# Bonus products three steps later, and the norms' products in another PSUM bank

## The chip, the cores and the metric

The kernel runs on one core of a Trainium2 chip. Times are microseconds (us) on the device, from the first to the last instruction of one execution with what lies around them. Matmuls run on TensorE (PE), elementwise work on VectorE (DVE), ScalarE (ACT) and GpSimd (POOL); SyncE (SP) and ACT issue the transfers. The engines run side by side, each through its own list of instructions in order, and wait for one another by semaphores. TensorE accumulates into PSUM banks, which the other engines read out.

## The reference

Two layers over 2048 tokens of width 1024, everything in float32. Layer 0 is RWKV-7 time mixing: shifted inputs are projected to r, k, v and g, a decay and a removal rate come from small LoRA products, and a recurrence over the tokens updates one 64 x 64 state for each of 16 heads. Beside the state's output each token gets a bonus from its own key and value:

```
y = ((y - mu) * lax.rsqrt(var + GN_EPS)).reshape(B, S, D) * ln_g + ln_b
bonus = jnp.sum(r * k * r_k, axis=-1, keepdims=True) * v
y = (y + bonus.reshape(B, S, D)) * jax.nn.silu(g)
```

Then one K and one V are projected from the residual stream, after a norm over each token. Layer 1 is attention with three groups of query heads (windows 128, 512 and 2048, with strides 1, 4 and 16) over this K and V, merged by their softmax sums, gated and projected back.

## The kernel before

A float32 product is done as three products of halves that the PE takes at full rate (`mm3`, L73 to L75: high times high, low times high, high times low). The kernel has three phases.

**Phase 1** (to about 1085 us) projects r, k, v and g, over four blocks of 512 tokens each. One step of this dense work is one slice of the contraction, into two banks: six products of 128x512. Beside it the loop drives a background: `run()` does 16 preps, `prep(v, hb)`, for eight blocks `v` of 256 tokens and two halves `hb` of the heads. A prep goes on by one yield in each dense step, and the tuple `W` (L37) says how many steps it waits between its stages. The stages of one prep:

- the second LoRA products L531 and L532, first for the decay (tile `sw`, weights `wa`), then for the removal rate (tile `tha`, weights `wb`); ACT takes each tanh of them, L535
- on DVE the running sum of the decays L537 and L540, on ACT their exponentials L544 and L545
- the products L550 that spread the keys' norms, and DVE's L553 to L559 which normalise and scale the keys
- POOL's L565, and L568 which writes r times k over the tile `kn`; on DVE L566, L570 and L569, which write the tiles `ar` and `bk`
- 64 pairs of short products of `ar` and `bk`, 32x32 each, L583 (called block products here); ACT copies their bank out, L599, into a tile of the pool slot of `sw`; two steps later they are stored to `abD`, L591
- the bonus: four products of `kn` with the weights r_k, L606, a copy on ACT, L608, and two steps later the turn, two transposes L614, which DVE's L618 copies into `beta`

All PSUM banks of the preps come from a pool of three, named "z". The tile `sw` has one buffer, so the tanh of the next prep waits until `abD` is stored.

Short things are not issued at once. A queue `tiny` holds them, and `sprinkle(2)` issues two after each pair of dense products. `later(steps, f, "prep")` puts f on a list of due times, counted in dense steps; `catch_up` issues what is due, and `catch_up("prep")` all of that name at once. Another background, the eliminations L640 and L642 (a triangular inverse by rows), runs on DVE and POOL between the preps.

**Phase 2** (about 1085 to 1780 us) runs the recurrence in chunks of 64 tokens and projects its output. The first chunk starts with L882.

**Phase 3** projects K, V, three sets of queries and the gate (jobs "k", "v", 2, 1, 0, "gate"), and runs the attention beside it. A job's products go into a pool of two banks, "ps". K's rows are turned by transposes L1458 into the one bank "tr", ACT copies them out (L1478) and issues their stores itself (L1472, and the larger L1481 with 16 values in a row). V's banks are copied out by ACT in L1486. Between the last token block of K and the one before the last of V, each block's tokens are scaled for the layers that follow: `rstd(tb)` spreads the 256 norms over all partitions by two products with the identity (L1331) into the bank "tr", ACT copies them out (L1334), POOL multiplies (L1318), DVE scales and shifts (L1322), and ACT issues the store `xbT` (L1324).

What stands where in an engine's list is not the order of the program text: a list scheduler takes the program in text order, keeps a model of each engine and of the banks, and orders each engine's list by it.

Of the kernel before, what the change touches and what calls it, by code (L numbers as in the profile page):

```python
# [9 lines left out]
F32 = mybir.dt.float32  # L10
# [5 lines left out]
P = 128  # L16
# [33 lines left out]
class Trunk:  # L50
# [148 lines left out]
    def phase1(self, keep):  # L199
# [17 lines left out]
        with ExitStack() as ctx:  # L217
# [12 lines left out]
            pz = bpool("pz", 3, space=PSUM)  # L230
# [227 lines left out]
            tiny, elims, due = deque(), deque(), []  # L458

            def sprinkle(n):  # L460

                while tiny and n:
                    tiny.popleft()()
                    n -= 1
# [5 lines left out]
            def catch_up(which=None):  # L470
                for d in sorted(due, key=lambda d: d[0]):
                    if d[0] <= now[0] or which in (d[2], "all"):
                        due.remove(d)
                        d[1]()

            def open_prep():
# [27 lines left out]
                def wait(n):  # L504
                    for _ in range(n):
                        yield
# [16 lines left out]
                def prep(v, hb, hr, kt, rt):  # L523
                    sw, tha = tile("sw"), tile("tha")
                    for i, dst in ((0, sw), (1, tha)):
                        for g in range(2):
                            z = pz.tile([P, 2, 256], F32, name="z")
# [18 lines left out]
                    for g in range(2):  # L546
                        z = pz.tile([P, 2, 256], F32, name="z")
# [10 lines left out]
                    nc.vector.scalar_tensor_tensor(k2, k2, 1.0, kt, op0=ALU.add, op1=ALU.mult)  # L558
                    nc.vector.scalar_tensor_tensor(tha, tha, 1.0, kn, op0=ALU.add, op1=ALU.mult)  # L559
                    yield from wait(W[3])  # L560
                    sprinkle(99)
                    catch_up("prep")
                    ar, bk = big("ar"), big("bk")
# [47 lines left out]
                    def turn(bo):  # L611
# [3 lines left out]
                        for s in range(2):  # L615
                            for c in range(2):
                                dst = self.beta[rows[1 - s]].rearrange("p (b c) j -> p c b j", c=2)
                                nc.vector.tensor_copy(dst[:, c, 2 * v:2 * v + 2, 4 * hb:4 * hb + 4], z[rows[c], :, :, s])  # L618
                    tiny.append(bonus)

                def eliminate(v, tiles=None):

# [39 lines left out]
                def run():  # L662
                    for v in range(NV):
                        for hb in range(2):
                            while v >= 2 * keys[0]:
                                yield
                            tiles = loads(v, hb)
                            yield from wait(W[0])
                            yield from prep(v, hb, *tiles)
                            yield from wait(W[6])  # L670
                    sprinkle(99)
# [554 lines left out]
    def phase3(self, keep):  # L1226
# [8 lines left out]
        with ExitStack() as ctx:  # L1235
            pool = lambda name, bufs, **kw: ctx.enter_context(tc.tile_pool(name=name, bufs=bufs, **kw))
            kept = self.kept
            wst, pp, pt, xb_, xp = (kept[n] for n in ("wst", "pp", "pt", "xb", "xs"))
# [6 lines left out]
            def two(which):  # L1245
                n = {"yp": "yc", "zp": "zc"}[which]
                return kept[which].tile([P, 2, 256], F32, name=n)
# [25 lines left out]
            def later(n, fn):  # L1273
                todo.append((clock[0] + n, fn))
# [51 lines left out]

            def rstd(tb):

                rp = pt.tile([P, 2, P], F32, name="tr")
                for i in range(2):  # L1330
                    mm(rp[:, i], self.rstd1[:, 2 * tb + i:2 * tb + i + 1].to_broadcast([P, P]), self.ident,  # L1331
                       start=True, stop=True)
                rb[tb] = two("zp")[:, 0]
                nc.scalar.activation(rb[tb], rp.rearrange("p a b -> p (a b)"), AF.Copy)  # L1334
# [180 lines left out]
            def project():  # L1515
# [3 lines left out]
                for n in range(8 * len(JOBS)):  # L1519
# [6 lines left out]
                    for s in range(32):  # L1526
                        gi, kc = divmod(s, KC)
                        half, i = divmod(gi, 2)
                        if s == 0 and (p, tb) >= (0, 7) and (p, tb) < (1, 7):
                            rstd((tb + 1) % 8)  # L1530
# [288 lines left out]
```

## Time and profile before

| what | value |
|---|---|
| median of 3 runs (lowest, highest) | 3774.16 us (3762.01 to 3776.55) |
| profiled execution | 3778.42 us |
| its span | 3776.5 us |
| mean granted clock of PE | 0.972 |
| PE busy | 3604.4 us, 95% of the span |
| DVE, ACT, POOL busy | 2481.2, 1809.5, 1437.8 us |

PE's share of 95% says that the whole kernel is a matter of how PE's list is fed. The span is 1.9 us shorter than the execution's time. The clock is given as a share of PE's full speed; 0.972 is the mean over the span, and single stretches show 1.00 or 0.50. The three runs lie 14.5 us apart.

### The profile page before, as it was taken

How to read it: one execution, taken by the hardware profiler on the slowest of the kernel's cores; microseconds unless marked ns; L12 is line 12 of the kernel's file. 1: busy time of each engine (PE TensorE's matmuls, PEld its weight loads, DVE VectorE, ACT ScalarE, POOL GpSimd, SP SyncE). 2: the span in 40 equal slices, each digit the busy share in tenths (PEclk: the TensorE clock that was granted, in tenths of full speed). 3: DMA queues.
4: the chain of work that ended last, by engine and by line, in shares of the span. 5: the costliest groups of instructions: out<-in, count | busy, mean ns of one | idle time of the engine just before them, and what ended most of it. 6: DMA issues, size and time to landing. Idle time of an engine off the chain costs nothing. (4 is left out here: it accounts for less than half of the span.)

```text
span 3776.5 us, 79506 instructions
## 1 busy us (share of the span) xinstructions
PE 3604.4 (95%) x29328; PEld 2863.5 (76%) x29328; DVE 2481.2 (66%) x6055; ACT 1809.5 (48%) x4638; POOL 1437.8 (38%) x1317
## 2 busy tenths in 40 slices
PE   7899999999999999998998999899999999999998
PEld 5565666676677999897776777677777788887888
DVE  4884467879877666765774367777866654464555
ACT  4554444344335444444443244466666665564441
POOL 3342355555535444443552244533422310042232
PEclk9899999999989999999999999999999999999999
DMA  8774555766665555544667455655654555465655
GB/s 276 229 235 136 155 161 174 205 193 191 182 155 141 120 118 123 123 102 127 126 128 177 144 124 81 137 158 143 193 142 130 146 156 143 151 190 173 183 162 172
DMA packets 1027124, 595.28 MB, mean 158 GB/s; under 512 B 564912, under 2 KB 918576, under 8 KB 1020592
## 3 DMA queue, kind: packets, MB, share of 16 engines
q1 hardware_dynamic: 629040, 500.00, 47.6%
q10 hardware_dynamic: 397696, 90.20, 11.3%
q8 instruction: 232, 3.80, 0.4%
q14 instruction: 156, 1.28, 0.1%
HBM read 391.84 MB, written 198.18 MB: 156 GB/s over the span
## 5 line engine op out<-in xcount | busy, mean ns | idle before, releaser
L1653 ACT ACTIVATE yt<-yt,nm 128x256 f32<-128x256 f32 (+1 forms) x768 | 345.1, 451 | 296.0 <-DVE nm L1649 295.5
L73 PE MATMUL ps<-xh,wh 128*128 128x512 f32 (+1 forms) x1248 | 451.0, 371 | 8.7 <-ACT xh L359 7.4
L74 PE MATMUL ps<-xl,wh 128*128 128x512 f32 (+1 forms) x1248 | 450.7, 362 | 4.0 <-DVE xl L361 2.8
L75 PE MATMUL ps<-xh,wl 128*128 128x512 f32 (+1 forms) x1248 | 446.9, 359 | 0.0
L73 PE MATMUL ps<-xh 128*128 128x512 f32 (+1 forms) x1152 | 422.1, 366 | 5.8 <-ACT ov L1486 3.4
L75 PE MATMUL ps<-xh,xl 128*128 128x512 f32 (+1 forms) x1152 | 402.5, 349 | 0.0
L74 PE MATMUL ps<-xl,xh 128*128 128x512 f32 (+1 forms) x1152 | 401.9, 349 | 0.0
L1208 POOL TENSOR_TENSOR rr_st<-rr_st,mh 128x8 f32<-128x8 f32 x128 | 223.1, 1743 | 455.3 <-DVE rr_st L1207 396.7
L73 PE MATMUL ps<-wh,xh 128*128 128x512 f32 x896 | 369.9, 413 | 10.4 <-ACT xh L66 5.2
L75 PE MATMUL ps<-wh,xl 128*128 128x512 f32 x896 | 359.5, 403 | 8.7 <-DVE xl L67 8.6
L74 PE MATMUL ps<-wl,xh 128*128 128x512 f32 x896 | 358.3, 400 | 0.5 <-DVE wl L1287 0.5
L73 PEld LDWEIGHTS ps<-xh,wh 128*128 128x128 f32 x1248 | 239.7, 194 | 82.4 <-issue 36.8
L1646 DVE CUSTOM_DVE_ANT_0 yt<-sc,amask 128x256 f32<-128x256 f32 (+1 forms) x768 | 237.2, 360 | 83.9 <-PE sc L1641 78.2
L74 PEld LDWEIGHTS ps<-xl,wh 128*128 128x128 f32 x1248 | 242.4, 194 | 59.5 <-issue 18.8
L75 PEld LDWEIGHTS ps<-xh,wl 128*128 128x128 f32 x1248 | 242.0, 194 | 51.1 <-issue 21.2
L73 PEld LDWEIGHTS ps<-xh 128*128 128x128 f32 x1152 | 220.7, 192 | 53.1 <-issue 19.6
L75 PEld LDWEIGHTS ps<-xh,xl 128*128 128x128 f32 x1152 | 220.5, 191 | 28.0 <-issue 0.3
L74 PEld LDWEIGHTS ps<-xl,xh 128*128 128x128 f32 x1152 | 221.2, 192 | 23.6 <-POOL xl L1292 0.4
L1213 POOL TENSOR_TENSOR rr_a<-rr_sq,TCS 128x512 f32<-128x512 f32 x128 | 183.9, 1437 | 109.1 <-DVE rr_sq L1211 90.1
L279 DVE SCALAR_TENSOR_TENSOR t<-hx,vecs,t 128x512 f32<-128x512 f32 x192 | 167.4, 891 | 84.5 <-ACT t L278 84.4
L73 PEld LDWEIGHTS ps<-wh,xh 128*128 128x128 f32 x896 | 171.3, 191 | 58.3 <-ACT xh L66 11.1
L1216 DVE TENSOR_TENSOR q<-rr_sq,TCS 128x256 f32<-128x256 f32 x256 | 211.0, 865 | 2.7
(341 smaller groups left out, 8604.7 us busy)
## 6 DMA issues: line engine op xcount, KB each, us to landing
hx<-hT SPq DMA_DIRECT2D x152, 256.5 KB
xb<-xbT SPq DMA_DIRECT2D x256, 128.0 KB
x<-Q SPq DMA_DIRECT2D x96, 256.0 KB
kq<-K SPq DMA_DIRECT2D x72, 256.0 KB
st<-in_w_in SPq DMA_DIRECT2D x64, 256.0 KB
arD<-ar SPq DMA_DIRECT2D x32, 512.0 KB
bkD<-bk SPq DMA_DIRECT2D x32, 512.0 KB
ls<-arD SPq DMA_DIRECT2D x64, 256.0 KB
```

Of the source, the lines that this page charges most:

```text
L73: i = mm(out, lh, rh, start=first, stop=False, **kw)
L74: mm(out, lh, rl, start=False, stop=False, **kw)
L75: mm(out, ll, rh, start=False, stop=last, **kw)
L279: nc.vector.scalar_tensor_tensor(t1, hx[:, 0:512], self.vec["a_mix_mu"][:, m:m + 1], t1, op0=ALU.mult, op1=ALU.add)
L1208: nc.gpsimd.tensor_tensor(st[:, 1], st[:, 0], mh, op=ALU.pow)
L1213: nc.gpsimd.tensor_tensor(a, sq, TC[:, tt, None, :].to_broadcast([P, 8, 64]), op=ALU.mult)
L1216: nc.vector.tensor_tensor(v[:, :, lo:lo + 32], sq[:, :, hi:hi + 32], TS[:, tt, None, lo:lo + 32].to_broadcast([P, 8, 32]), op=ALU.mult)
L1646: nc.vector.tensor_tensor_reduce(out=u.pr[:, h, :nk], in0=sc[h][:, x, :nk], in1=amask[:, int(g == 0), 256 - nk:256], scale=1.0, scalar=-3e ...
L1653: nc.scalar.activation(u.pr[:, h, :nk], u.pr[:, h, :nk], AF.Exp, bias=nm[:, x, h:h + 1], accum_out=lm[:, x, h, 0:1])
```

## The change

It has two parts. First, at the end of a prep the bonus is no longer put on `tiny` at once but three dense steps later; a second `catch_up("prep")` ahead of the block stage makes sure that it is on `tiny` before `sprinkle(99)` empties that. Second, the products that spread the norms take a bank of the pool `pz` (two banks, "z"), which phase 2 used and phase 3 uses again only in the attention.

```
...
                     yield from wait(W[3])
+                    catch_up("prep")
                     sprinkle(99)
                     catch_up("prep")
...
-                    tiny.append(bonus)
+                    later(3, lambda: tiny.append(bonus), "prep")
...
             def rstd(tb):
 
-                rp = pt.tile([P, 2, P], F32, name="tr")
+                rp = kept["pz"].tile([P, 2, P], F32, name="z")
                 for i in range(2):
...
```

One line is added at L561, so later lines of the changed kernel have a number one higher: the block products are L584, the bonus L607, the turn L615.

PE's list at the end of a prep in the middle of phase 1, before: the block products, the bonus, the first LoRA products of the next prep (`hr` is their input), and the turn behind the second four.

```order
L583 MATMUL z<-ar,bk 32x32 x64
L606 MATMUL z<-kn,rkb 32x256 x4
L531 MATMUL z<-hr,wa 128x256
L532 MATMUL z<-hr,wa 128x256
...
L74 MATMUL ps<-xl,wh 128x512
...
L532 MATMUL z<-hr,wa 128x256
L614 MATMUL z<-cst,bo 128x128 x2
L75 MATMUL ps<-xh,wl 128x512
```

The same place in the changed kernel: all eight LoRA products and 17 dense ones stand between the block products and the bonus, and 21 dense ones between the bonus and the turn (21 to 26 in other preps).

```order
L584 MATMUL z<-ar,bk 32x32 x64
L531 MATMUL z<-hr,wa 128x256
...
L532 MATMUL z<-hr,wa 128x256
L74 MATMUL ps<-xl,wh 128x512
...
L75 MATMUL ps<-xh,wl 128x512
L607 MATMUL z<-kn,rkb 32x256 x4
L73 MATMUL ps<-xh,wh 128x512
...
L75 MATMUL ps<-xh,wl 128x512
L615 MATMUL z<-cst,bo 128x128 x2
```

PE's list at the end of phase 1, before, from the last prep's block products on (`pd` is the bank of the last gate's products, the last projections of phase 1): 21 dense products stand between the bonus and the turn, and 19 more behind the turn.

```order
L74 MATMUL ps<-xl,wh 128x512
L583 MATMUL z<-ar,bk 32x32 x64
L606 MATMUL z<-kn,rkb 32x256 x4
L75 MATMUL ps<-xh,wl 128x512
...
L74 MATMUL ps<-xl,wh 128x512
L614 MATMUL z<-cst,bo 128x128 x2
L75 MATMUL ps<-xh,wl 128x512
```

The same place in the changed kernel, from the turn of the prep before the last on (`wb` are the weights of `tha`, `s` holds the norms): the last prep's `tha`, norms, block products, bonus and turn stand with one dense product between them, and then the products into `pd`.

```order
L615 MATMUL z<-cst,bo 128x128 x2
L531 MATMUL z<-hr,wb 128x256
...
L532 MATMUL z<-hr,wb 128x256
L75 MATMUL ps<-xh,wl 128x512
L550 MATMUL z<-hr,s_3120 128x256 x4
L584 MATMUL z<-ar,bk 32x32 x64
L607 MATMUL z<-kn,rkb 32x256 x4
L615 MATMUL z<-cst,bo 128x128 x2
L73 MATMUL pd<-xh,wh 128x512
```

ACT's list where K ends and V begins, before: a store of K (L1481), a store of scaled tokens (L1324), and the copy of the spread norms behind them.

```order
L1486 ACTIVATE ov<-ps,rstd_71 128x512 x2
L1286 ACTIVATE xh<-st,vecs 128x512
L1472 DMA K_20796<-sg 128x4x128
L1481 DMA K_20797<-x 8192x1x16
L1324 DMA xbT<-yc 128x256
L1334 ACTIVATE zc<-tr 128x256
L1487 DMA V<-ov 128x512 x2
```

The changed kernel there: four of the stores of scaled tokens stand ahead of V's first copy out of a bank "ps" (now L1487), and the store of K ahead of its second one. Five of the eight pairs of spreading products stand earlier, in the tail of phase 2.

```order
L1325 DMA xbT<-yc 128x256
L1325 DMA xbT<-xb 128x256
...
L1487 ACTIVATE ov<-ps,rstd_71 128x512
L1482 DMA K_20797<-x 8192x1x16
L1488 DMA V<-ov 128x512
L1487 ACTIVATE ov<-ps,rstd_71 128x512
L1335 ACTIVATE zc<-z 128x256
```

## Rows read from the trace of the kernel before

**Rows 1.** PE's waits, 400 to 1090 us: waits summed, times, longest, in us

```profile
PE z L606 <- POOL kn L568: 16.5, 7, 4.2
PE z L583 <- DVE bk L569: 5.1, 3, 3.2
PE z L531 <- DVE beta L618: 3.5, 2, 3.3
PE z L882 <- DVE o L443: 3.4, 1, 3.4
...
PE z L882 <- DMA bk<-bkD: 0.8, 1, 0.8
```

**Rows 2.** Timeline of PE, 626 to 642: start, us, instruction, [idle before, releaser]

```profile
626.37 1.29 PE L583 MATMUL z<-ar,bk 64*32 64x32 f32 x128
631.85 1.08 PE L606 MATMUL z<-kn,rkb 128*32 128x256 f32 x8 [4.19 <-POOL kn L568]
...
641.01 0.38 PE L532 MATMUL z<-hr,wa 64*128 64x256 f32 x1
641.32 0.44 PE L614 MATMUL z<-cst,bo 128*128 128x128 f32 x2
```

**Rows 3.** Table of stretches: length, busy time by engine, PEclk, DMA share

```profile
583.60:590.20 6.60, 5.61 (x18) 3.42 (x19) 3.32 (x9) 0.38 (x1) 0.94 (x1) 0.50 0.71 216
...
1027.40:1034.00 6.60, 6.60 (x16) 4.78 (x16) 6.13 (x14) 0.21 (x1) 5.50 (x15) 0.50 0.82 223
...
1062.00:1068.00 6.00, 6.00 (x27) 4.67 (x25) 4.80 (x17) 0.44 (x1) 0.00 (x0) 1.00 0.99 276
...
900.00:1000.00 100.00, 96.89 (x775) 72.89 (x774) 91.10 (x173) 38.25 (x68) 37.81 (x51) 0.96 0.67 190
```

**Rows 4.** Timeline of POOL, 570 to 640

```profile
573.71 10.83 POOL L568 TENSOR_TENSOR kn<-rt,k 128x1024 f32<-128x1024 f32 x1 [8.58 <-DVE tmp L640]
...
629.27 2.52 POOL L568 TENSOR_TENSOR kn<-rt,k 128x1024 f32<-128x1024 f32 x1
...
632.19 0.36 POOL L640 TENSOR_TENSOR tmq<-u,el 128x40 f32<-128x40 f32 x1
```

**Rows 5.** Line L568: what POOL waited for before it, us and times

```profile
  DVE ar L566: 55.4, 6
```

**Rows 6.** Timeline of PE: block products of the last two preps

```profile
1022.12 1.29 PE L583 MATMUL z<-ar,bk 64*32 64x32 f32 x128
...
1068.16 1.29 PE L583 MATMUL z<-ar,bk 64*32 64x32 f32 x128
```

**Rows 7.** Timeline of ACT: the last prep's tanh of sw

```profile
1036.16 1.57 ACT L535 ACTIVATE sw<-z,zb 128x256 f32<-128x256 f32 x4 [8.55 <-DMA abD<-sw]
```

**Rows 8.** Timeline of DVE, 1036 to 1076: the last prep

```profile
1038.72 2.33 DVE L540 TENSOR_TENSOR_SCAN sw<-cst,sw 128x512 f32<-128x512 f32 x2
...
1061.50 1.21 DVE L569 SCALAR_TENSOR_TENSOR bk<-tha,sw 128x1024 f32<-128x1024 f32 x1
...
1075.37 0.70 DVE L618 COPY beta<-z 64x8 f32<-64x8 f32 x4 [5.88 <-PE z L614]
```

**Rows 9.** PE's waits, 1940 to 2100 us

```profile
PE tr L1331 <- ACT x L1478: 5.0, 1, 5.0
PE tr L1331 <- ACT zc L1334: 4.8, 1, 4.8
```

**Rows 10.** Timeline of ACT, DMA issues (ACTq) included, 1984 to 2032

```profile
1997.67 0.52 ACTq L1481 DMA_DIRECT2D K<-x  x1
...
1998.29 7.13 ACTq L1324 DMA_DIRECT2D xbT<-yc  x1
...
2016.18 0.55 ACTq L1481 DMA_DIRECT2D K<-x  x1
...
2019.46 5.13 ACTq L1324 DMA_DIRECT2D xbT<-yc  x1
```

**Rows 11.** Timeline of PE: products that spread the norms

```profile
2017.04 0.61 PE L1331 MATMUL tr<-cst,rstd 128*128 128x128 f32 x4
```

More of the change, by code (lines that the diff above doesn't have):

```diff
@@ L560, in prep @@
                     yield from wait(W[3])
+                    catch_up("prep")
                     sprinkle(99)
@@ L618, in turn @@
                                 nc.vector.tensor_copy(dst[:, c, 2 * v:2 * v + 2, 4 * hb:4 * hb + 4], z[rows[c], :, :, s])
-                    tiny.append(bonus)
+                    later(3, lambda: tiny.append(bonus), "prep")
                 def eliminate(v, tiles=None):
@@ L1327, in rstd @@
             def rstd(tb):
-                rp = pt.tile([P, 2, P], F32, name="tr")
+                rp = kept["pz"].tile([P, 2, P], F32, name="z")
                 for i in range(2):
```

## The prediction

> **What bounds the kernel now.** I read the page's first two parts first: TensorE (PE) is busy for 95% of the span, so only time in which PE stands still, or runs at its lower clock, can be won or lost. Then I read PE's waits in the stretch from 400 to 1090 us, where the short products run in the background of the input projections [rows 1]. The reader is to see that one line leads: L606, the bonus products, waits for kn written by L568 on GpSimd (POOL), 16.5 us in 7 waits, the longest 4.2; there are 16 such places, one for each prep. VectorE (DVE) causes most of the rest: 5.1 us before the block products L583, 3.5 us before the LoRA products L531 (for beta, L618), 3.4 us before the first chunk L882.
>
> Third, PE's rows around one such wait [rows 2]: the 128 block products start at 626.37 and end at 627.66, then PE stands 4.19 us until 631.85, when kn has come. Fourth, the table of stretches [rows 3], for the clock. After four of the seven waits (near 584, 632, 714 and 1027; first and last shown) the granted clock is 0.50, the lower of the two levels (1.2 GHz), over a stretch of 6.6 us; in 1062 to 1068, after a long stretch without a wait, it is 1.00 with 27 products in 6.0 us, 0.222 us each. At half speed 6.6 us hold 3.3 us of work, so each such stretch costs 3.3 us beside its wait.
>
> Last, PE's waits around 2000 us, where the shared K ends and V begins [rows 9]: the products that spread the tokens' norms (L1331) wait there 5.0 and 4.8 us for the bank "tr".
>
> **Part 1: the bonus products three steps later.** Removed: the order of before puts them right behind the 64 pairs of block products. In the new order eight LoRA products and 17 dense products stand between. By rows 2 a LoRA product takes 641.32 - 641.01 = 0.31 us, so 8 x 0.31 + 17 x 0.222 = 6.3 us lie between. The longest of the seven waits was 4.2. POOL's own order has L568 some eight elimination rows later in several preps; such a row took 0.36 us [rows 4], so this takes up to 8 x 0.36 = 2.9 us of the cover back, and leaves 3.4 where POOL is late already. That is still nearly as long as the longest wait, and I count all seven as gone: -16.5. With them go the four stretches at half clock, 4 x 3.3 = -13.2, if nothing else makes PE stand at the same place. Sum -29.7; if the clock falls there all the same, -16.5.
>
> One row speaks against a fixed lead: L568 took 2.52 us at 629.27 but 10.83 us at 573.71 [rows 4], while DVE ran beside it. The Trainium skill, "GPSIMD Engine Reference", section "1. Specifications", says that GpSimd's interface to SBUF is shared with VectorE and that instructions of VectorE with two inputs in SBUF contend with it. The trace agrees with the long case, and by that rule a lead can be eaten whenever such VectorE work falls beside L568; the wait would then be 10.8 less 6.3 at worst, once.
>
> What is late next: the turn (L614) and the second half of the LoRA products (tha) move with the bonus. In the new order the turn stands 21 to 26 products behind the bonus, some 12 us behind the blocks, and tha right behind it; tha needs the bank that beta (0.70 us on DVE, rows 8) frees, and sw's tanh, which waits for the store abD of the blocks. I cost eight such waits of 0.7 at +5; against it stand the 5.1 us before L583, since each prep now spans some 3 us more of dense products. These two I let cancel, with 5 either way in the range.
>
> **Part 1, the other side: the last prep.** The preps now take more dense products each, and the dense products do not grow. In the order before, the last prep's blocks stand among the last projections, and at 1068.16 [rows 6], and some 40 dense products come behind them. In the new order, behind the blocks of the prep before the last there stand 16 LoRA products, 17 + 21 + 1 dense ones, one bonus and one turn, and then the last prep's key norm and blocks with nothing dense ahead of them. That cover is 16 x 0.31 + 39 x 0.222 + 0.64 + 0.4 + 0.5 = 15.2 us. The chain that must fit into it is read from before: those blocks end at 1022.12 + 1.29 = 1023.41 [rows 6]; the next sw tanh starts at 1036.16, released by the store abD [rows 7], 12.8 us later; L569, the last input of the last blocks, ends at 1061.50 + 1.21 = 1062.71 [rows 8], 26.5 us after that. The second piece was stretched in before by PE's own order and by neighbours on DVE; its lower bound is up to the scan's end (1038.72 + 2.33 - 1036.16 = 4.9), three us for tha's tanh and the key norm, and six DVE passes of 1.21, 15.2 in all. I take the middle, 21. Uncovered: 12.8 + 21 - 15.2 = 18.6, with ends of 12.8 and 24.1. From it goes the wait of L882 (3.43 + 0.76 = 4.2, rows 1), which runs out in the meantime; to it come 0.6 us for bonus, bo and turn now one behind the other, and one stretch at half clock, 3.3. Net +18.3 (12 to 24).
>
> **Part 2: the norms' products take another bank.** Two products and one ACT copy per block are the same as before; four of them take 0.61 us [rows 11]. Five of eight pairs now stand in the tail of phase 2, where they may push a product behind them: +1 at most 2. The waits of rows 9 go, -9.8, with two stretches at half clock, -6.6. But the bank was not the cause: ACT was [rows 10]. These rows show ACT's DMA issue behind the K store of L1481: 1997.67 the store, then 7.13 us for the next issue L1324; 2016.18 the store, then 5.13 us. ACT stands for that time, whatever the bank. In the new order V's own evacuation L1486 stands behind four such issues and again behind an L1481, so PE's next accumulation waits for its ps bank in place of tr. The two ps banks hide at most one group of 24 products, 24 x 0.222 = 5.3 us. I take three stalls now, 7.1 + 5.1 less what is hidden of a third, and with the clock about 20 us for the 16.4 that go: +4. Ends: -16 (all hidden) and +15 (three of 7.13 with their stretches, 3 x 10.4 = 31 less 16.4).
>
> The Trainium skill, "DMA: Bandwidth & Descriptors", section "Issuing engines are not separate DMA queues", says that issuing on several engines only saves the sequencer's time to issue, usually small against the DMA itself. Rows 10 differ: 7.13 us of the issuing engine. By the page the stall would be nothing and part 2 would bring its full 16.4; by the rows it is moved.
>
> **Sum** against the profiled execution's own 3778.42 us (span 3776.5): -29.7 + 18.3 + 1 + 4 = -6.4, 3772.0. That execution lies 4.3 above the median of the runs, 3774.16, so I forecast 3768.
>
> **Rivals.**
> Faster: the last prep's chain takes its lower bound (with its ends 12.8 uncovered, net 12), and the K/V stalls are hidden behind ps banks: -29.7 + 12 + 1 - 16.4 = -33, about 3741. For it: beside the last prep there is no more dense work to evacuate, so ACT and DVE are freer than in rows 7 and 8. Against it: the ACT issues stand in the order as before.
> Slower: VectorE bounds the stretch, not GpSimd. In 900 to 1000 us DVE is busy 91.10 of 100 us [rows 3], and L568 itself waits 55.4 us in six places for DVE's ar, L566 [rows 5]. If DVE's total sets phase 1, PE's waits only move, from L606 to L583, L531 and tha, and nothing of the 29.7 comes; the uncovered last prep stays: +18.3 + 1 + 4 = +23, about 3797. It decides as soon as PE's waits on DVE in 400 to 1060 grow from 14 us by more than some 24 us. Against it: PE's waits on DVE are shorter than those on POOL, and DVE still has 9 us of 100 free.
> No gain from the move: the bonus wait turns into a wait of the turn or tha for sw's tanh or beta, half of the 16 preps at 2 us, while the clock recovers in two of four places: -29.7 + 16 + 7 + 23 = +16, about 3790. The 8.55 us that ACT waited for abD in rows 7 speaks for it; against it, that tha comes later now too.
>
> **How the numbers follow.** Under 0.5% (19 us) a measurement of this kernel cannot tell a difference from none. My forecast, between 3756 and 3787, has 0.49; the faster rival 0.25 with all of it below 3755; the slower rival 0.19 with most beyond 3793; no gain 0.07, inside 0.5%. That makes faster 0.25, same 0.56, slower 0.19. The best sum of ends is -34.8 + 12 - 16 = -39, 3735, the worst -16.5 + 24 + 15 + 2 = +25, 3799; 8 times in 10 I expect 3742 to 3796. The forecast's own range is 3756 to 3787.
>
> **What would show it.** Right: no wait of L607 (the bonus's new line) in 440 to 1035; granted clock 1.00 behind the blocks near 584, 632, 714; a wait of 12 to 24 us of the last blocks L584 near 1050, with DVE and ACT busy on the last prep alone; no wait for tr of the norms' products, but waits of ps for L1487 behind 5 to 7 us issues on ACT near 1990 to 2030. Wrong: waits of L584, L531 and tha for DVE grown by as much as L607's went, or last blocks that find their inputs ready.

## The result, and the profile after

The changed kernel takes 3800.61 us (median of 6 runs, 3799.58 to 3802.96) against 3770.68 for the kernel before (6 runs, 3754.58 to 3776.55). The ratio is 1.0095, 95% interval 1.0080 to 1.0109: slower by 36 us (30 to 41); the two medians lie 29.9 us apart. The forecast was 3768, no change that can be told; its range ended at 3796.

The page of the changed kernel, its first part and PE's clock in 40 slices: PE is busy 14 us longer for the same instructions, and the clock of the twelfth slice (1045 to 1140 us) is down to 0.70, the 6 in its row.

```profile
PE 3618.8 (95%) x29328; PEld 2870.8 (76%) x29328; DVE 2498.9 (66%) x6055; ACT 1806.6 (48%) x4638; POOL 1428.9 (38%) x1317
...
PEclk9899999999968999999998999999999999999999
```

PE's waits between 400 and 1110 us, the answer to [rows 1]. The waits for kn are gone. The longest wait is that of the last block products, and the first chunk waits for a load. Where a row says "issue", the profile shows nothing that the engine waited for. One wait is new at the bonus itself: at 804.8 us L607 stands 6.1 us for L600, ACT's copy of the blocks, whose bank the bonus now takes.

```profile
PE z L584 <- DVE tmp L641: 13.1, 1, 13.1
PE z L550 <- issue: 8.1, 4, 4.5
PE z L883 <- DMA ls<-arD: 8.0, 1, 8.0
PE z L607 <- ACT sw L600: 6.1, 1, 6.1
PE z L531 <- ACT sw L535: 3.4, 2, 2.1
```

PE's timeline at the end of phase 1, the answer to [rows 6]: the last key norm, blocks, bonus and turn, and the first chunk L883. PE stands 3.18, 13.05, 0.50 and 8.04 us between 1074.5 and 1109.0, 24.8 us in all.

```profile
1077.72 0.89 PE L550 MATMUL z<-hr,s 4*128 4x256 f32 x4 [3.18 <-issue]
1091.66 1.93 PE L584 MATMUL z<-ar,bk 64*32 64x32 f32 x128 [13.05 <-DVE tmp L641]
1093.53 1.08 PE L607 MATMUL z<-kn,rkb 128*32 128x256 f32 x8
1095.11 0.65 PE L615 MATMUL z<-cst,bo 128*128 128x128 f32 x2 [0.50 <-ACT bo L609]
1109.02 2.04 PE L883 MATMUL z<-ls,bk 64*128 64x128 f32 x8 [8.04 <-DMA ls<-arD]
```

The profile puts the 13.05 us down to L641, which came last, but the input that came last is bk from L570: DVE ends it at 1091.52. Ahead of it in DVE's list stand 3.4 us of work for phase 2 (L1114, L939), which the blocks don't need.

```profile
1086.79 2.31 DVE L1114 TENSOR_SCALAR hgate<-adaA 128x8 f32<-128x8 f32 x1
1089.15 1.11 DVE L939 MEMSET x<- 64x512 f32 x2
1090.29 1.23 DVE L570 SCALAR_TENSOR_TENSOR bk<-tha,sw 128x1024 f32<-128x1024 f32 x1
```

What the first chunk waits for stands in the lists of DVE and SP. DVE's clearing of the tile ls (L826) waits 8.39 us for the last prep's store abD; SP issues that store at 1100.20 and the load of ls at 1104.95, behind it.

```profile
1104.88 0.48 DVE L826 MEMSET ls<- 64x512 f32 x1 [8.39 <-DMA abD<-sw]
```
```profile
1100.20 2.41 SPq L592 DMA_DIRECT2D abD<-sw  x4
...
1104.95 1.36 SPq L852 DMA_DIRECT2D ls<-arD  x2
```

To see where the time goes I cut each trace at the same dense products (those of `mm3`, counted from the start): stage A from the 1081st to the 2881st, the background preps; stage B from there to the 3121st, the end of phase 1 and the first chunks. The table of stretches (columns as in [rows 3]) for before, for the second part alone (whose program is that of before in stage A), and for the changed kernel:

```profile
424.10:1055.01 630.91, 599.22 (x4248) 430.54 (x4247) 509.41 (x887) 262.94 (x473) 333.53 (x381) 0.95 0.62 178
1055.01:1227.58 172.57, 158.29 (x2251) 134.28 (x2249) 123.53 (x320) 71.04 (x173) 76.55 (x95) 0.90 0.68 159
```
```profile
421.44:1045.54 624.10, 598.04 (x4247) 430.22 (x4247) 508.74 (x887) 262.18 (x473) 326.00 (x381) 0.95 0.63 180
1045.54:1225.65 180.11, 164.88 (x2252) 139.90 (x2250) 125.45 (x320) 71.23 (x173) 76.18 (x95) 0.87 0.68 152
```
```profile
423.48:1040.19 616.71, 591.63 (x4089) 424.67 (x4089) 487.41 (x827) 251.72 (x457) 310.41 (x355) 0.95 0.61 177
1040.19:1267.14 226.95, 189.81 (x2409) 157.26 (x2408) 157.61 (x382) 79.25 (x189) 95.18 (x122) 0.79 0.58 137
```

In stage A the changed kernel is 7 to 14 us shorter, but PE does 6 to 8 us less there: 159 instructions of the late preps have moved to stage B. PE stands still (length less busy time) for 25.1 us against 31.7 and 26.1. So next to nothing was won; with the bonus alone moved it is 32.0 us. In stage B it is 47 to 54 us longer: it stands 37.1 us against 14.3 and 15.2; about 7 us of moved work; and the rest, 18 to 25 us, goes with the clock, 0.79 against 0.90 and 0.87. All traces here show only the two levels 1.00 and 0.50, so a mean of 0.79 over 227 us means 2 x 0.21 x 227 = 95 us at half clock, against 35 and 47. Both stages together take 843.7 against 803.5 and 804.2 us.

Where K ends and V begins, PE's waits from 1975 to 2130 us, the answer to [rows 9]: none for the norms' products, but 5.3 us for V's copies L1487 and 5.4 for the bank tr of K's transposes.

```profile
PE tr L1459 <- ACT x L1479: 5.4, 3, 2.6
PE ps L73 <- ACT ov L1487: 5.3, 2, 3.9
```

ACT's list there, the answer to [rows 10]: the long issues are still there, 6.70 and 6.71 us behind a store L1482, and the next copy out of a ps bank stands behind the second one.

```profile
2021.68 0.53 ACTq L1482 DMA_DIRECT2D K<-x  x1
2024.32 6.70 ACTq L1473 DMA_DIRECT2D K<-sg  x1
...
2035.68 0.56 ACTq L1482 DMA_DIRECT2D K<-x  x1
2038.17 6.71 ACTq L1488 DMA_DIRECT2D V<-ov  x1
...
2044.92 0.69 ACT L1487 ACTIVATE ov<-ps,rstd 128x512 f32<-128x512 f32 x1 [8.72 <-PE ps L75]
```

From there to about 3390 us the lag of the changed kernel behind the profiled execution of before stays between 30 and 33 us. In its last stretch that execution of before is 6 to 13 us longer than all other traces, so the two spans end only 22.0 us apart. Single executions differ by some 10 us in stage A alone (620.8, 624.1 and 630.9 for programs that are the same there, the first but for its last prep), so ratios are taken from the timed runs.

### The profile page after: what moved, and what is told of

Read it like the earlier page. It is cut to its first block, busy times and chain, and to the rows that moved or that the text cites. A ratio compares the mean times of both kernels' runs of the same rounds, so it can differ in the third digit from the quotient of the medians.

```text
span 3798.5 us, 79500 instructions
## 1 busy us (share of the span) xinstructions
PE 3618.8 (95%) x29328; PEld 2870.8 (76%) x29328; DVE 2498.9 (66%) x6055; ACT 1806.6 (48%) x4638; POOL 1428.9 (38%) x1317
## 5 line engine op out<-in xcount | busy, mean ns | idle before, releaser
L75 PE MATMUL ps<-wh,xl 128*128 128x512 f32 x896 | 362.5, 406 | 12.8 <-DVE xl L67 12.1
L75 PEld LDWEIGHTS ps<-xh,wl 128*128 128x128 f32 x1248 | 240.7, 193 | 47.6 <-issue 17.6
L75 PEld LDWEIGHTS ps<-wh,xl 128*128 128x128 f32 x896 | 171.8, 192 | 61.8 <-DVE xl L67 21.7
```

The lines of the kernel that those rows point to most:

```text
L75: mm(out, ll, rh, start=False, stop=last, **kw)
```

## The experiments

All ratios are against the kernel before, run beside it on the same chip.

**Either part alone.** `bonus_only` has the first part's two lines alone, `rstd_only` the second's one line.

> Only the first part of the change: the bonus three steps later, the norms' products in the old bank. Theory T1 (the last prep): the whole loss sits at the end of phase 1, where the last prep now stands behind all dense products, so this is as slow as the whole change, ratio 1.007 to 1.011 against before, PE's wait before the last block products 10 to 16 us. Theory T2 (the norms' bank): the loss comes from the five pairs of norm products that moved into the tail of phase 2 and from V's copies behind ACT's issues, so this is no slower than before, 0.992 to 1.000. Theory T3 (VectorE bounds phase 1): as slow as the whole change too, but PE's waits between 440 and 1060 us then sum to as much as before's, about 27 us, without the bonus in them.

> Only the second part: the norms' products in a bank of the pool pz. T1 and T3: between 0.997 and 1.001 of before, since the lag of the changed kernel moved by only -3 us around the end of K. T2: 1.005 or more.

Measured: the bonus alone 1.0082 (1.0065 to 1.0098), the norms' bank alone 0.9977 (0.9963 to 0.9991), that is -9 us (-14 to -3). The loss belongs to the first part: T2 falls. T3's sign did come: PE's waits from 440 to 1060 us sum to 34.2 us with the bonus alone and to 27.2 in the whole change, against 31.5 before, without a wait for kn in them. The two ratios multiply to 1.0059, while the whole change measured 1.0095; the 14 us between them (8 by the medians) are not explained. In the trace of the second part alone the two waits of [rows 9] are replaced by three for V's copies and three for K's bank, 13.6 us for 9.8, while all of PE's waits from 1940 to 2100 us sum to 17.6 us against 19.8:

```profile
PE ps L73 <- ACT ov L1487: 8.0, 3, 4.8
PE tr L1459 <- ACT x L1479: 5.6, 3, 2.2
```

Cut at the same dense products, the 5201st to the 6501st (about 1920 to 2280 us), the five traces with the norms in the old bank take 353.8 to 356.4 us there, and nine of the ten with the new bank 350.0 to 354.7 (the other 365.0). So some 3 of the 9 us lie there; where the others come from is not settled.

**Is it the turn's bank?** The three banks z go round. Before, the bonus took the bank behind the blocks and the turn one that was free. With the bonus moved behind eight LoRA products, the turn is next for the bank that sw's first products hold until ACT's tanh, and that tanh waits for the store abD. `change_turn_bank` gives the turn another bank:

```
+            def spare():
+                if stage[0] >= 8:
+                    return pq.tile([P, 512], F32, name="ssp")
+                return pz.tile([P, 512], F32, name="z")
...
-                        z = pz.tile([P, 2, 4, 32], F32, name="z")
+                        z = spare()[:, 0:256].rearrange("p (b j r) -> p b j r", b=2, j=4)
...
+                stage[0] = n
```

> The whole change, and from the v projection on the turn (two transposes of the bonus) takes the one bank of the key norms' sums, which is free then, in place of one of the three banks z. PE's order then has the bonus still 17 dense products behind the blocks, but a prep spans about 112 dense products again and some 43 stand behind the last blocks. T1: the waits for the bonus are gone and the last prep is covered, so 16 to 30 us faster than before, ratio 0.991 to 0.997, first chunk at about 1060 to 1075 us. T3: the waits move to VectorE's results, ratio 0.999 to 1.006. If the turn's bank had nothing to do with it: as slow as the change, 1.008 or more.

Measured: 1.0015 (1.0006 to 1.0025). Against the whole change's 1.0095 that is some 30 us back, so the bank is what leaves the last prep bare. But it is not faster than before: T1 was right on the end and wrong on the bonus waits, and the ratio lies in T3's range. No wait for kn is left among PE's waits from 440 to 1060 us, and others stand there:

```profile
PE z L589 <- DVE bk L575: 6.3, 3, 4.4
PE ps L74 <- DVE xl L361: 6.0, 2, 4.5
PE z L536 <- ACT sw L540: 5.0, 2, 2.5
```

**More preps left bare.** `change_three_late` has one step less between preps, with which the scheduler's order comes out the other way:

```
-W = (2, 3, 3, 3, 4, 2, 1)
+W = (2, 3, 3, 3, 4, 2, 0)
```

> The whole change with one step less between the preps (last number of W 0 in place of 1). In PE's order not one but the last three preps then stand behind all dense products of phase 1. T1: three chains with nothing beside them, of some 25 to 35 us each where the change has one, so 40 to 75 us slower than the change, ratio to before 1.018 to 1.030. T3: the engine that bounds does the same work, so within 10 us of the change, 1.006 to 1.012.

Measured: 1.0152 (1.0134 to 1.0169), 21 us beyond the change: the direction of T1, but less than its range and more than T3's. The table shows why: stage A is 34 us shorter than in the change, since much of the preps' work has left it, and stage B, 54 us longer, pays more than that back, at a clock of 0.75.

```profile
422.25:1005.32 583.07, 562.09 (x3910) 409.65 (x3910) 433.41 (x733) 246.61 (x438) 247.39 (x287) 0.98 0.61 174
1005.32:1286.31 280.99, 199.55 (x2589) 159.75 (x2588) 196.34 (x473) 88.20 (x207) 128.72 (x189) 0.75 0.57 137
```

**What is a bonus wait worth?** In `no_pool_wait`, the order of before is kept but for small shifts and the wait is made needless:

```
-                            mm(z[32 * j:32 * j + 32], rkb[:, 4 * hb + j], rk[:, j], start=True, stop=True)
+                            mm(z[32 * j:32 * j + 32], rkb[:, 4 * hb + j], rt[:, j], start=True, stop=True)
```

> The kernel before, and the bonus products read r in place of r times k, so that they wait for nothing from GpSimd; L568 is still computed (the bonus is then not the reference's). The order stays nearly that of before: the bonus right behind the blocks, 42 dense products behind the last blocks. Theory T1 (the waits for kn are worth their own length and their half clock): 16 to 30 us faster, ratio 0.992 to 0.996. Theory T3 (behind the wait stands VectorE, and the time moves to other waits): within 6 us of before, 0.9985 to 1.0015, with PE's waits for VectorE and ACT between 440 and 1060 us up by 10 us or more.

Measured: 0.9986 (0.9970 to 1.0001), -5 us (-11 to 0), where T1 asked for -16 to -30; it lies in T3's range. PE's waits from 440 to 1060 us in this run:

```profile
PE ps L74 <- DVE xl L361: 4.8, 1, 4.8
PE z L583 <- DVE bk L569: 3.7, 2, 2.0
PE z L531 <- ACT sw L535: 3.2, 2, 2.6
PE z L531 <- issue: 2.4, 1, 2.4
PE z L531 <- DVE beta L618: 2.4, 2, 1.4
PE z L531 <- DVE u L642: 2.2, 1, 2.2
PE z L531 <- ACT sw L599: 2.1, 1, 2.1
```

The LoRA products L531, next behind the bonus, wait 12.3 us in place of 7.7: what the bonus had waited, they now wait in part. All waits of that window sum to 21.8 us against 31.5. In stage A PE stands 21.9 us, against 26.1 to 31.7 in three traces with the bonus waits. Stage A takes 616.6 us here, 4 to 14 less than in those three; stage B takes 181.7 at a clock of 0.85, against 172.6 at 0.90 before and 180.1 at 0.87 with the second part alone. So part of the gain may have gone again in stage B, but the spread of single executions is as large, and this is not shown.

**A bare end without moving the bonus.** `last_prep_late` holds back only the last prep:

```
-                            yield from wait(W[0])
+                            yield from wait(W[0] + (30 if (v, hb) == (NV - 1, 1) else 0))
```

> The kernel before, and only the last prep begins 30 dense steps later. Order of the first 15 preps as before; the last prep's LoRA products have some 90 dense products before its blocks, so little of its chain is bare, but nothing dense is left behind its blocks. If the whole loss of the change is the bare chain before the last blocks (13 us): within 5 us of before. If, as I now think, much of it is what stands behind, the first chunk's loads that wait for the last prep's store, and the half clock after it: 12 to 28 us slower, ratio 1.003 to 1.0075, first chunk waiting 6 to 15 us for a load.

Measured: 1.0032 (1.0014 to 1.0050), 12 us (5 to 19), at the lower end. The first chunk waits for its load, but 2.9 us, not 6 to 15:

```profile
PE z L882 <- DMA ls<-arD: 2.9, 1, 2.9
```

Its last blocks find their inputs ready, and 23 dense products stand between them and the first chunk, against 58 before and 18 in the change. So a last prep with little behind it costs about 12 us even when its chain is covered; in the change the bare chain comes on top.

**Turn's bank without moving the bonus.** `before_both_banks` is the kernel before with `spare()` for the turn and the second part.

> The kernel before with the bonus in its old place, the norms' products in pz, and the turn in the key norms' free bank. PE's order then has preps of about 105 dense products and some 150 behind the last blocks. T1: bonus waits as before, an end better covered: 0.995 to 0.999. T3: VectorE's work is pressed into a shorter stretch, so PE's waits before the blocks and for beta grow by what the earlier end brings: 0.997 to 1.003.

Measured: 1.0023 (1.0010 to 1.0036), slower than the second part alone (0.9977) although some 150 dense products stand behind the last blocks. It lies in T3's range. More than the 40 of before brought nothing here, and the preps, packed tighter, make PE wait elsewhere: 9.8 us for kn still, 6.5 for the copy of the blocks, 5.8 for bk.

**Covering the end with useless work.** At the end of `run()` the two `change_filled` kernels issue what is still on `tiny` and due, and then add products that nothing reads (120, or 80):

```
...
+                    z = pq.tile([P, 512], F32, name="ssp")
+                    for _ in range(120):
+                        mm(z, wl2[0][:, 0:P], wl2[1][:, 0:512], start=True, stop=True)
```

> The whole change, and 120 products of 128x512 of two constant weight tiles into a free bank, which nothing reads: 120 x 0.222 = 26.6 us of extra work for TensorE. In PE's order they stand around the prep before the last, and push 43 real dense products behind the last blocks. Theory T1 (the change's loss of some 30 us is the bare end of phase 1 with its half clock): the end is covered as in before, so 26.6 slower than before at most, and 5 to 25 us faster than the change itself although it does more: ratio to before 1.001 to 1.007, granted clock 1.00 around the last blocks and the first chunk's wait as before. If the loss is spread over phase 1 or lies elsewhere: the extra work comes on top, 1.014 to 1.017.

> As the run with 120 products, with 80 (17.8 us of extra work): 11 dense products behind the last blocks in PE's order, all others ahead of them. T1: the chain before the blocks is covered, the first chunk's wait for its loads only in part; ratio to before 1.001 to 1.006. Loss elsewhere: 1.012 to 1.015.

Measured: 120 products 1.0103 (1.0085 to 1.0121), 80 products 1.0075 (1.0058 to 1.0091). With 26.6 us of useless work the kernel is as slow as the change, and with 17.8 us it is not slower than it. If the useless products cost their full length, the kernels would have been 12 and 10 us slower than before without them. So the end accounts for some 25 us of the change's loss, by that estimate, and about 10 us remain; both ratios lie between the two expectations. The first chunk still waits 4.9 and 8.7 us in them, against 3.4 before. Stage B is back at its old length in the run with 120:

```profile
1073.06:1249.57 176.51, 162.12 (x2252) 137.94 (x2250) 122.43 (x308) 73.04 (x177) 75.44 (x95) 0.88 0.68 152
```

**Is VectorE the bound?** `before_light_dve` leaves adds out:

```
-                            eng.tensor_tensor(u[:, a:e, m + 1:], u[:, a:e, m + 1:], tm, op=ALU.add)
+                            if a or v == NV - 1:
+                                eng.tensor_tensor(u[:, a:e, m + 1:], u[:, a:e, m + 1:], tm, op=ALU.add)
```

> The kernel before, and VectorE leaves out its adds L642 of the eliminations of all blocks of tokens but the last (their result is then not the reference's): some 92 us less for VectorE between 500 and 1050 us, with the bonus in its old place in all preps but one and 45 dense products behind the last blocks. T3 (VectorE's list is what PE's waits come from in the end): L568 and the preps' DVE passes come earlier, PE's waits between 440 and 1060 fall by 10 us or more, ratio 0.990 to 0.997. If the bonus waits come from GpSimd's own work: within 4 us of before.

Measured: 1.0010 (0.9995 to 1.0026). The adds of some 92 us are gone, and since the rest of VectorE's work took longer, it is busy for 53 us less in stage A (456.81 us, against 509.41). There is no gain from that, and of PE's waits from 400 to 1160 us four for kn remain:

```profile
PE z L606 <- POOL kn L568: 11.6, 4, 4.1
```

T3, that VectorE's total sets phase 1, falls. What stays of it is that the waits move: its ranges held in `change_turn_bank`, `no_pool_wait` and `before_both_banks`.

**Cutting the other link.** What was still open was why the waits are worth so little. Three kernels give the copied block products a tile of their own, so that the next tanh need not wait for abD:

```
-                    ab = tile("sw")[:, 0:2].rearrange("p a t -> p (a t)").rearrange("p (j c i) -> p j c i", c=4, j=4)
+                    ab = ep.tile([P, 512], F32, name="ab").rearrange("p (j c i) -> p j c i", c=4, j=4)
```

> The whole change, and the copy of the block products (ab) gets a tile of its own in place of the buffer of sw, so that the next prep's tanh need not wait for the store abD. PE's order then has the bonus 17 dense products behind the blocks, a prep spans about 115 dense products, and 40 stand behind the last blocks. Theory T1 (the turn claims the bank that sw's LoRA products hold until that tanh, so the store abD sets the length of a prep and the last prep is left bare): 24 to 45 us faster than the change, 0.996 to 1.002 of before. If the price is the three steps' delay itself and not the store: as slow as the change, 1.007 to 1.010. If the bonus's old waits had only hidden the wait for sw: PE's waits for kn, sw and L531 together below 8 us between 440 and 1060, and 10 us or more faster than before, 0.994 to 0.9975.

> The second part of the change only, with ab in a tile of its own. Bonus at its old place; in PE's order preps span about 106 dense products and some 144 stand behind the last blocks. If the store abD is what PE waits for behind the bonus waits: faster than the second part alone (0.9977), 0.992 to 0.996. If the bonus waits stay and only the end changes: 0.996 to 0.999.

> The whole change with ab in its own tile and the turn in the key norms' bank: neither a bank nor the store abD ties one prep to the next. PE's order has preps of some 104 dense products and 180 behind the last blocks, the bonus 14 to 29 dense products behind its blocks. If bank and store are all that stood in the way of the bonus's gain: the fastest of all, 0.990 to 0.995. If the time is VectorE's and ACT's results anyway: 0.997 to 1.003, with waits for bk (L570) and sw's tanh in their place.

Measured: on the whole change 0.9991 (0.9977 to 1.0005), on the second part alone 1.0009 (0.9994 to 1.0023), and with the turn's bank too 0.9988 (0.9975 to 1.0001). The first takes some 39 us off the change, so the chain of bank, tanh and store is shown from both its ends: cutting either link covers the last prep. In the first, PE's waits from 440 to 1060 us have no kn and no sw in them, but the turn now waits for bo and the bonus for the copy ab:

```profile
PE z L615 <- ACT bo L609: 6.5, 5, 2.2
PE z L550 <- issue: 6.4, 1, 6.4
PE z L607 <- ACT ab L600: 3.9, 3, 1.8
```

But the 10 us or more beyond before did not come, nor the 0.990 to 0.995 of the third, which lies in its other range: its waits are 9.6 us for the copy ab, 7.0 for sw's tanh and 2.9 for bk. The second lies outside both of its ranges; it waits 10.6 us for kn and 9.3 for bk. Of all these the second part alone has the lowest ratio, 0.9977, though its interval overlaps with those of the first and third.

## Why the prediction was wrong

**The waits for kn, -29.7.** The waits did go: no L607 waits for POOL. This step failed in what it took them to be worth. Made needless with little else changed, they brought 5 us (0 to 11). PE's list in phase 1 goes through one wait after another for the same prep: blocks, bonus, LoRA products, turn, key norm. What stands in it is late against the same few results on ACT, DVE and POOL, so a wait taken out at one place comes up in part at the next. Stage A has 21 to 36 us of standing in all fifteen kernels traced, with or without waits for kn. These sums are measured; that the same few results hold the list up is argued, not shown. The 13.2 us for the clock did not come either: 0.95 in stage A before, 0.95 after.

**New waits for bank and tanh, cancelled against L583.** The step saw that the turn needs sw's tanh, and priced the wait at 0.7 us each. The waits for that tanh stayed small, as priced (two, 3.4 us in all). A wait that the step didn't have came at the bonus, 6.1 us for ACT's copy of the blocks; "no wait of L607" was one of the signs of being right, and it failed there. What the tie of bank and tanh did was to lengthen the preps, which the order showed and the next step used.

**The last prep, +18.3 (12 to 24).** Place and kind were right: 13.05 us before L584 and 3.18 before L550, 16.2 together, where 18.6 were forecast. Two terms behind it failed. The step let L882's 4.2 us run out during the wait; instead the first chunk waited 8.04 us, since its loads wait for the last prep's own store. And it put 3.3 us for one stretch at half clock; stage B has 95 us at half clock where 35 to 47 were, worth 18 to 25 us. Over both stages the end cost about 40 us by the trace, twice the forecast.

**The norms' bank, +4 and +1.** Right that the long issues on ACT stay and now hold V's copies. The sum had the wrong sign, -9 us measured, inside the ends of -16 and +15. The Trainium skill ("DMA: Bandwidth & Descriptors", "Issuing engines are not separate DMA queues") says that the sequencer's time to initiate a DMA is usually small relative to the DMA itself. In this place it is not small: 6.70 and 6.71 us after, 7.13 and 5.13 before; how long these DMAs themselves took, no row here shows.

**The rivals.** The slower one gave 3797, nearest to 3800.6. Its shape was right, no gain in phase 1 and the bare last prep, but that the number is so near is in part luck: its 18.3 for the end was some 40, and its +5 for the second part was -9. Its cause, VectorE's total, did not stand the lighter VectorE, and its own sign did not come: PE's waits on DVE from 440 to 1060 us fell from 10.8 to 4.5 us, where they should have grown by 24. The case that the waits only move had a chance of 0.07 and is what phase 1 did, though not to the turn and tha in the main, but to the bonus's new bank and to waits that the profile gives no name (L550, L531: 8.0 us). The faster rival had the bare chain at its lower bound, 12.8 us; it was 16.2.

**What stays open.** Which result is the last to bound a prep in phase 1; the 14 us by which the whole change is slower than the product of its parts; and the 10 us that the filled kernels and, against 0.9977, the change with the turn's bank (14 us) still lose with the end covered.

## What to carry to other kernels

A wait of the engine that bounds is worth its length only if the next instruction in its list has its inputs by then; make the wait needless in a throwaway kernel before counting on it. When short work is moved behind other short work that shares a ring of banks, look at who now inherits which bank and what its last reader waits for. And price the end of a background chain with all that stands behind it, the next phase's loads into the same memory and the clock included.

## What the runs showed of the hardware

PE stood still for 24.8 us between 1074.5 and 1109.0 (the four waits above). In the changed kernel the granted clock was 0.50 (1.2 GHz) from 1075.1 to 1095.6, with PE busy for 4.32 us; 1.00 to 1105.8, in which the gate's products into `pd` ran; and 0.50 again to 1150.2, 44.4 us, although PE did not stand any more from 1109.0 on and was busy for 41.18 of them.

```profile
1075.10:1095.60 20.50, 4.32 (x142) 2.94 (x142) 18.08 (x34) 3.26 (x8) 3.67 (x4) 0.50 0.90 227
1095.60:1105.80 10.20, 4.50 (x19) 3.30 (x18) 1.41 (x6) 0.00 (x0) 0.87 (x3) 1.00 0.77 215
1105.80:1150.20 44.40, 41.18 (x363) 34.35 (x365) 22.71 (x58) 7.16 (x19) 16.94 (x45) 0.50 0.37 81
```

Before, the clock was 0.50 for 17.1 us there, from 1088.7 to 1105.8. The first 63 us from the first chunk on, before and then changed: 0.86 with 61.15 us busy, 0.67 with 62.98 us busy and 101 instructions fewer done.

```profile
1087.00:1150.00 63.00, 61.15 (x841) 51.39 (x842) 48.98 (x135) 24.76 (x62) 28.46 (x48) 0.86 0.80 172
```
```profile
1109.00:1172.00 63.00, 62.98 (x740) 52.72 (x742) 42.19 (x126) 18.30 (x47) 25.47 (x52) 0.67 0.41 89
```

What an issue behind a store of K (L1481, changed L1482) costs ACT depends on how soon it comes. In the traces of both kernels 19 issues come 0.6 to 6.8 us behind the start of such a store; they take 1.7 to 7.1 us, and all end 6.7 to 9.4 us behind that start. The 13 that come 10 us or more behind it take 0.34 to 0.37 us. So the issue takes what is left of some 7 to 9 us, and where other work filled 10 us behind the store it cost ACT nothing more than usual.
